# A hybrid recurrence and convolution layer on one core: where the modulation sums leave their bank, the order of the first squares, and the place of the gate sums

## The chip, the core and the metric

The kernel runs on one core of a Trainium2 chip. The core has a matrix engine (PE; PEld is its loading of weights), a vector engine (DVE), a scalar engine (ACT), a general engine (POOL) and a sequencer that issues most transfers (SP). The metric is the device time of one execution in microseconds. Three runs of the kernel before took 2156.95 to 2159.48 us, median 2158.66.

## What is computed

One layer over 2048 latent tokens `x` of width 1024, with 256 context tokens `ctx` in front (in short form):

```python
shift, scale, gate = split(silu(c) @ w_ada + b_ada, 3)          # and the same from c_ctx
h  = rmsnorm(x, norm_w) * (1 + scale) + shift                   # hc from ctx likewise
p  = h @ w_in                                                   # 1024 -> 9216 columns
pc = hc @ w_in[:, :5120]
# 8 heads of 128: q, v, forward and backward forget gates, output gate;
# a gated linear recurrence in both directions, which starts from the context's final states
y_hg = rms(o) * onorm_w * silu(p_gate)
# 1024 channels: u = cg * h_, a convolution over 3 neighbours in rows of 64
y_cv = bg * conv3(u) * silu(p_cgate)
y = concat(y_hg, y_cv) @ w_out
out = rmsnorm(x + gate * y, final_norm_w)
```

`shift` and `scale` are needed before anything else can be multiplied with `w_in`; `gate` is needed only at the very end, in the residual addition.

## The kernel before

**Tiling.** The tokens stand in four groups of 512 (`NG = 4`), the model width in eight blocks of 128 partitions (`KT = 8`, `HK = 4`). Large products are made of float16 pairs (a high and a low part), three matmuls for each product, and by a scheme of seven block products in place of eight (`seven`). The operands of a group for that scheme are the seven "hop" tiles B11, T1, T2, B21, T3, B22, T4. They are built once, stored to device memory (`Hd0` to `Hd3`), and loaded again (`hop_tile`) for each stretch of work that uses that group. Groups 0 and 1 are first used in a plain form (`plain`), and their T products are built later, by the eight "late turns" (`late_turn`), which read the saved rows `Xd` back.

**Stages.** The opening computes the sums for `shift` and `scale` (`modulate`, bank `pada`, 128x512), copies them out and transposes them (`modulate_end`), adds the bias (`ada`), and makes from them the columns `ab` with which every transposed row of the tokens is scaled and shifted (`affine`, `rows`). For group 0 the raw transposed rows already stand in SBUF (`raw`); so `rows` only scales them in place, on DVE for the first four blocks and on ACT for the last four. Then `turn` makes the high and low parts.

After that runs a list of windows (`stretch`): head 0 by its four token groups (windows 0 to 3), head 1 by its four groups in reverse order (windows 4 to 7), and so on, then the convolution and the output. Window 0 also multiplies the context. Each window has its products on PE (`units`), a chain of steps for the scan of the segment before (`scan_steps`, `context_steps`), and extra steps.

**What sets the order.** Each step has a weight (`PACE`, `paced`). The two lists of a window are merged by the share of their weight done (`merge_steps`), and `run` issues a step when the products have come that far. Instructions are written down in this order with a priority, and a scheduler then fixes each engine's queue before the run; it may draw an instruction forward when its inputs and its buffer are free. So an engine's queue is fixed and runs in order, but not always in the order of the list. `follow` pins some instructions behind a given one on their engine.

**The extra steps of windows 0 to 2.** For each following group there are five lists from `norm_group`: loads, squares and `norm` (the sum of squares by ACT, then a reciprocal root by small DVE steps, then the scaling, split between DVE and ACT), turns, late turns, and rows made ahead. In window 0 the order is: the context's squares and norm (`ctx_norm[1]`), its turns, the loads of group 2, the squares and norm of group 1 (`n1[1]`), its turns. In window 2, group 3 is turned, each turn with the next turn's rows ahead. Windows 3 to 6 make two late turns each.

**Gate sums.** `gate_sums` loads the third 1024 columns of `w_ada` in eight tiles of 512 KB (`wg`, in tiles of the pool that holds the Q tiles, six slots), multiplies each with the conditioning columns `sc32` into one bank, copies the bank out and stores it (`Gr`) for the end. Before, it is an extra list of window 3: two loads, then by turns one `part` and one load.

**Pools.** Three banks of PSUM serve transposes and the scan's level products (`pa_t`), two serve values, keys, states and scales (`px_t`), three the large products (`bank`).

**Loads of hop tiles.** `prefetch` keeps a queue of the hop tiles that windows will need, in order, nine slots in all. It issues a load when a slot is free and the group's operands are ready (`ready`, `late_done`). Windows 3 and 4 share group 3; window 5 loads group 2 again.

Of the kernel before, what the change touches and what calls it, by code (L numbers as in the profile page):

```python
# [14 lines left out]
AF = mybir.ActivationFunctionType  # L15
ALU = mybir.AluOpType
# [5 lines left out]
KT = D // P  # L22
# [4 lines left out]
NG = SEQ // GW  # L27
NCH = GW // P
HK = KT // 2
HW = GW // 2  # L30
# [20 lines left out]
def paced(weight, fn):  # L51

    return PACE.get(weight, weight), fn


def sub(t, off, dims):
    return bass.AP(t.tensor, t.offset + off, [list(t.ap[0])] + [list(d) for d in dims])
# [3 lines left out]
def hybrid_layer(ctx: ExitStack, tc, x, cx, w_ada, b_ada, w_in, w_out, fnorm_w, small_d, masks, ident_d, sel_d, out):  # L61
    nc = tc.nc
    V, S, G, PE, SY = nc.vector, nc.scalar, nc.gpsimd, nc.tensor, nc.sync
# [30 lines left out]
    def pa_t(nm):  # L94
        return pa.tile([P, 512], F32, tag="pa", name=nm)

    def px_t(nm):
        return px.tile([P, 512], F32, tag="px", name=nm)

    def ring(nm):  # L100
        return rp.tile([P, GW], F32, tag="ring", name=nm)
# [61 lines left out]
    par, at = {}, 0  # L163
# [8 lines left out]
    ab = cp.tile([P, 2, 2, KT], F32, name="ab")  # L172
# [39 lines left out]

    def modulate_end(pada):
        ada_r = ring("ada_r")
        V.tensor_copy(ada_r[:, :HW], pada[:, :HW])
        S.activation(ada_r[:, HW:], pada[:, HW:], AF.Copy)
        ptr = pa_t("ada_t")
        turned = [PE.transpose(ptr[:, q * P:(q + 1) * P], ada_r[:, q * P:(q + 1) * P], ident) for q in range(4)]
        V.tensor_tensor(ada, ptr.rearrange("p (q j m) -> p j q m", q=4, j=4)[:, :, :, 0:2],
                        sub(bada, 0, [[4, 4], [1, 4], [0, 2]]), ALU.add)  # L220
        return turned
# [20 lines left out]
    def norm_group(ntile, src, row0, m, nm, first_ops=None, space=q_tile):  # L242
# [29 lines left out]
        def transposed(k, space=pa_t):  # L272
            pt = space(f"xT_{nm}{k}")
            for i in range(ntile):
                PE.transpose(pt[:, i * P:(i + 1) * P], xs[i][:, k * P:(k + 1) * P], ident)
            return pt
# [9 lines left out]
        def rows(k):  # L286
            if k in raws:
                h32 = raws[k]
                if k < HK:
                    V.tensor_scalar(h32, h32, ab[:, m, 0, k:k + 1], ab[:, m, 1, k:k + 1], ALU.mult, ALU.add)  # L290
                else:
                    S.activation(h32, h32, AF.Identity, bias=ab[:, m, 1, k:k + 1], scale=ab[:, m, 0, k:k + 1])
                return h32
            pt = transposed(k)
            h32 = ring(f"h32_{nm}{k}")
            S.activation(h32[:, :n], pt[:, :n], AF.Identity, bias=ab[:, m, 1, k:k + 1], scale=ab[:, m, 0, k:k + 1])
            return h32
# [776 lines left out]
    def gate_sums():  # L1074

        pg, wa = [], {}

        def load(k):
            wa[k] = flat(q_tile(f"wg{k}"))
            SY.dma_start(wa[k], w_ada[0, k * P:(k + 1) * P, 2 * D:])  # L1080

        def part(k):
            if k == 0:
                pg.append(pa_t("gate_r"))
            for j in range(2):
                r = 64 * (k % 2) + 32 * j
                PE.matmul(pg[0][r:r + 32, :], sc32[:, k, :], wa[k][:, j * 512:(j + 1) * 512],
                          start=k < 2, stop=k >= KT - 2)

        def rows():  # L1090
            r = ring("gate_rows")
            S.activation(r, pg[0], AF.Copy)
            SY.dma_start(Gr, r)

        steps_ = [lambda: load(0), lambda: load(1)]
        for k in range(KT):
            steps_.append(lambda k=k: part(k))
            if k + 2 < KT:
                steps_.append(lambda k=k: load(k + 2))
        return [paced(1.0, f_) for f_ in steps_ + [rows]]  # L1100

    def gate_steps():
        t = {}
# [123 lines left out]
    for wi, (kind, a, i) in enumerate(stretch):  # L1227
        units, chain, extra = [], [], []
# [147 lines left out]
    queue = []  # L1376
    freed = [0]
    taken = [0]
    ready = [0]
# [3 lines left out]

    def prefetch():
        while (queue and taken[0] < freed[0] + HOPS and queue[0][1] <= ready[0]
               and late_done.get(queue[0][1], HK) == HK):
            wi_, g_, o = queue.pop(0)
            t = hop_tile(f"hop{wi_}{o}")
            SY.dma_start(t, Hd[g_][o])
            hop.setdefault(wi_, {})[o] = t  # L1390
            taken[0] += 1

    late_done = {0: 0, 1: 0}
    plain = [[hp.tile([P, 2, 2, GW], F16, tag="hop", name=f"hop{g}_{i}") for i in range(KT // 2)] for g in range(2)]
    x1_norm = norm_group(NCH, x, GW, 0, "x1", plain[1], stage_tile)
# [5 lines left out]
    first = norm_group(NCH, x, 0, 0, "x0", plain[0])  # L1401
# [9 lines left out]
    pada = modulate(lambda k: first[4][k]() if k < KT - 2 else None, lambda: next_w(0))  # L1411
    ctx_norm = norm_group(2, cx, 0, 1, "c")
# [11 lines left out]
    def store_plain(g):  # L1424
        for o in ("B11", "B21", "B22"):
            r, half = int(o[1]) - 1, int(o[2]) - 1
            for i in range(HK // 2):
                SY.dma_start(Hd[g][o][:, 2 * i:2 * i + 2],
                             plain[g][r * HK // 2 + i][:, :, :, half * HW:(half + 1) * HW])
# [107 lines left out]
    for wi, (units, chain, extra) in enumerate(windows):  # L1537
        if wi < NG - 1:
            n1 = x_norm[wi + 1]
            n2 = x_norm[wi + 2] if wi + 2 < NG else None  # L1540
            ready_ = [paced(0.0, lambda g=wi + 1: set_ready(g))]
            if wi == 0:
                more_params()
                early = ([paced(0.1, lambda: store_plain(0))] + ctx_norm[1] + ctx_norm[2] + n2[0] + n1[1] + n1[2]
                         + [paced(0.1, lambda: next_w(1, 6))] + n2[1] + ready_)
            elif wi == 1:
                x3 = [st for _, st in n2[0]]
                early = ([paced(0.1, lambda: store_plain(1))] + n1[2][:2] + [paced(0.0, x3[0]), paced(0.0, x3[1])]
                         + n1[2][2:3] + [paced(0.0, x3[2]), paced(0.0, x3[3])] + n2[1][:2] + n1[2][3:] + ready_
                         + n2[1][2:] + n2[5][:1])  # L1550
            else:
                early = [st for k in range(HK) for st in n1[2][k:k + 1] + n1[5][k + 1:k + 2]] + ready_
            extra = early + extra
        elif wi < NG + 3:
            n_ = (wi - NG + 1) * 2
            extra = (x1_norm[3] + first[3])[n_:n_ + 2] + extra
        if wi == NG - 1:
            extra = extra + gate_sums()
        if wi >= NG:
            ready[0] = NG  # L1560
        run(wi, units, merge_steps(chain, extra))
        if stretch[wi] == ("conv", 0, 1):
            close_scan()
        elif stretch[wi] == ("conv", 0, 3):
            afterwards.append(close_heads)
        elif stretch[wi] == ("pair", 7, 0):
            load_wo(0, 6)
            afterwards.append(lambda: load_wo(6, 7))
        elif stretch[wi] == ("pair", 7, 1):
            afterwards.append(lambda: load_wo(13, 14))  # L1570
# [113 lines left out]
```

## Time and profile before

| | us |
|---|---|
| median of three runs | 2158.66 |
| profiled execution | 2153.81 |
| its span | 2152.0 |
| PE busy | 2076.1 (96% of the span) |
| DVE busy | 1645.7 (76%) |
| ACT busy | 1192.0 (55%) |
| POOL busy | 184.7 (9%) |
| mean granted clock of PE | 0.994 |

The profiled execution is a single one; its own time is its span and 1.81 us around it. In the rows of the views, a time in square brackets is the idle time of the engine just before the instruction, with what ended it. "x4" means four instructions in a row merged into one line. In a row by tile, three numbers with slashes are the shortest, the median and the longest duration in ns. The granted clock is a share of PE's full speed. An instruction on PE, DVE or ACT starts a little before the end of the one ahead, so durations in a row add up to slightly more than the time they take.

### The profile page before, as it was taken

What the parts mean: (1) busy time and instruction counts of PE and PEld (TensorE: products, weight loads), DVE (VectorE), ACT (ScalarE), POOL (GpSimd) and SP (SyncE); (2) the same over time, 40 slices, a digit from 0 to 9 for tenths busy, and PEclk for the clock granted to TensorE, in tenths of its full rate; (3) what the DMA queues carried; (4) which work ended last, traced back from release to release, by engine and by line L of the source; (5) the groups of instructions that cost most, each with busy time, mean ns of one, the idle gap of its engine ahead of it and who ended that gap; (6) DMA issues with size and microseconds to landing.
All of it is one profiled execution on the core that took longest, in us unless ns stands there. A gap on an engine that the chain in (4) does not pass through costs nothing.

```text
span 2152.0 us, 53038 instructions
## 1 busy us (share of the span) xinstructions
PE 2076.1 (96%) x22111; PEld 1466.1 (68%) x22111; DVE 1645.7 (76%) x3415; ACT 1192.0 (55%) x2406; POOL 184.7 (9%) x271
## 2 busy tenths in 40 slices
PE   5988999999999999999999999999999999999998
PEld 2777778888888888888888887444444444444443
DVE  7787888878778787788787887678778656687775
ACT  6965666766567666667676654354445423333332
POOL 0121111011111110111110100000000000000000
PEclk8999999999999999999999999999999999999999
DMA  9557544442243333423633457933442105642421
GB/s 359 181 174 259 181 153 147 138 139 90 97 147 131 112 114 109 136 98 129 207 130 125 132 164 258 288 108 109 136 147 94 55 22 196 206 144 90 137 79 59
DMA packets 185797, 311.01 MB, mean 145 GB/s; under 512 B 13010, under 2 KB 114770, under 8 KB 183764
## 3 DMA queue, kind: packets, MB, share of 16 engines
q1 hardware_dynamic: 183396, 303.68, 42.6%
q8 instruction: 173, 2.83, 0.5%
q10 hardware_dynamic: 2160, 3.93, 0.5%
q14 instruction: 68, 0.56, 0.1%
HBM read 240.19 MB, written 67.37 MB: 143 GB/s over the span
## 4 chain that ended last, share of the span: by engine, by line
PE 64%; DVE 18%; ACT 8%; DMA 4%; issue 3%; POOL 1%; SPq 0%; POOLq 0%; ACTq 0%; DVEq 0%
PE sa L930 8%; PE sa L932 8%; PE sa L931 8%; PE sb L930 4%; PE sb L931 4%; PE sb L932 4%; PE sa_o L930 2%; PE sa_o L931 2%; PE sa_o L932 2%; DVE Q L492 2%; PE sc L930 2%; PE sc L931 2%; PE sc L932 2%; PE T L681 2%; DVE K L485 2%
## 5 line engine op out<-in xcount | busy, mean ns | idle before, releaser
L931 PEld LDWEIGHTS <-e_p 128*128 128x128 f16 x1332 | 130.3, 98 | 57.3 <-issue 8.1
L930 PEld LDWEIGHTS <-e_p 128*128 128x128 f16 x1332 | 130.3, 98 | 56.2 <-issue 3.6
L485 DVE TENSOR_TENSOR K<-K,tot 128x512 f32<-128x512 f32 x192 | 133.0, 693 | 45.7 <-ACT km L601 28.2
L932 PEld LDWEIGHTS <-e_p 128*128 128x128 f16 x1332 | 130.3, 98 | 51.0
L601 ACT ACTIVATE km<-K 128x512 f32<-128x512 f32 x192 | 129.6, 676 | 62.0 <-DVE K L485 58.2
L492 DVE TENSOR_TENSOR Q<-Q,tot 128x512 f32<-128x512 f32 x192 | 132.9, 692 | 35.5 <-POOL qm L608 19.4
L608 POOL COPY qm<-Q 128x512 f32<-128x512 f32 x96 | 79.1, 824 | 796.4 <-DVE Q L492 796.4
L931 PEld LDWEIGHTS <-whib_p 128*128 128x128 f16 x888 | 87.2, 98 | 39.7 <-issue 6.2
L930 PEld LDWEIGHTS <-whib_p 128*128 128x128 f16 x888 | 87.1, 98 | 37.9 <-issue 1.7
L931 PEld LDWEIGHTS <-whia_p 128*128 128x128 f16 x888 | 86.9, 98 | 36.7 <-issue 4.6
L932 PEld LDWEIGHTS <-wlob_p 128*128 128x128 f16 x888 | 87.1, 98 | 34.1
L930 PEld LDWEIGHTS <-whia_p 128*128 128x128 f16 x888 | 86.9, 98 | 34.1 <-issue 0.8
L932 PEld LDWEIGHTS <-wloa_p 128*128 128x128 f16 x888 | 86.9, 98 | 34.0
L157 ACT ACTIVATE e_p<-ws_p,sc_p 128x512 f16<-128x512 f32 x108 | 77.5, 719 | 53.8 <-DVE ws_p L444 39.2
L665 POOL COPY A<-Ac 32x128 f32<-32x128 f32 x128 | 75.8, 593 | 128.9 <-ACT A L661 119.4
L937 ACT ACTIVATE u<-sa,sx_w 128x256 f32<-128x256 f32 (+1 forms) x111 | 58.1, 524 | 47.2 <-PE sa L932 38.2
L853 ACT ACTIVATE cv<-c,small 128x512 f32<-128x512 f32 (+1 forms) x36 | 24.2, 673 | 106.0 <-DVE c L871 60.8
L937 ACT ACTIVATE p<-sa,sx_w 128x256 f32<-128x256 f32 (+1 forms) x111 | 57.5, 518 | 42.2 <-PE sa L932 42.2
L409 ACT ACTIVATE junk<-ws_p 128x1024 f16<-128x1024 f32 x72 | 75.7, 1052 | 5.7 <-DMA ws_p<-in_w_in 5.5
L158 DVE SCALAR_TENSOR_TENSOR e_p<-ws_p,sc_p,e_p 128x512 f16<-128x512 f32 x108 | 78.7, 743 | 0.0
L1595 POOL TENSOR_TENSOR x_o<-x_o,fw 128x512 f32<-128x512 f32 x1 | 1.3, 1262 | 868.4 <-ACT junk L1586 868.4
L937 ACT ACTIVATE p<-sb,sx_w 128x256 f32<-128x256 f32 (+1 forms) x111 | 57.9, 521 | 31.1 <-PE sb L932 28.5
(858 smaller groups left out, 7029.7 us busy)
## 6 DMA issues: line engine op xcount, KB each, us to landing
ws_p<-in_w_in SPq DMA_DIRECT2D x72, 512.0 KB, 4.3
y_o<-yT SPq DMA_DIRECT2D x32, 512.0 KB, 4.3
xt_x<-in_x SPq DMA_DIRECT2D x16, 512.0 KB, 5.9
wa<-in_w_ada SPq DMA_DIRECT2D x16, 512.0 KB, 10.2
Gd<-zs SPq DMA_DIRECT2D x32, 256.0 KB, 2.8
sg<-Gd SPq DMA_DIRECT2D x32, 256.0 KB, 3.9
wos<-in_w_out SPq DMA_DIRECT2D x32, 256.0 KB, 4.8
yT<-y SPq DMA_DIRECT2D x32, 256.0 KB, 2.7
```

Of the source, the lines that this page charges most:

```text
L157: S.activation(hi, src, AF.Copy, scale=st[:, 0:1])
L158: V.scalar_tensor_tensor(lo, src, st[:, 0:1], hi, ALU.mult, ALU.subtract)
L409: S.activation(junk.rearrange("p (k n) -> p k n", k=KT), stage[i], AF.Abs, accum_out=r)
L485: V.tensor_tensor(m, m, sub(cur, nb + 1, [[2, np_], [-(nb + 1), 2], [0, B]]), ALU.mult)
L492: V.tensor_tensor(m, m, sub(cur, 1, [[2, np_], [nb - 1, 2], [0, B]]), ALU.mult)
L601: S.activation(sub(s.km, 0, [[2 * B, n // (2 * B)], [B, 2], [1, B]]), mix(s.K, n, B, n // (2 * B)), AF.Copy)
L608: G.tensor_copy(sub(qm, 0, [[2 * B, n // (2 * B)], [B, 2], [1, B]]), mix(s.qf, n, B, n // (2 * B)))
L665: G.tensor_copy(A3[js, :, js], s.Ac[js])
L930: PE.matmul(ps, hi[:, k], rh, start=start and k == 0, stop=False, skip_group_check=not start)
L931: PE.matmul(ps, hi[:, k], right(name, 1, k), start=False, stop=False, skip_group_check=not start)
L932: PE.matmul(ps, lo[:, k], rh, start=False, stop=k == nk - 1, skip_group_check=not start)
L937: last_keep.append(S.activation(r, ps, AF.Copy, scale=sx))
```

## The change

Four edits, all within the first seven windows:

1. `modulate_end` copies the whole bank of modulation sums with one ACT copy instead of a DVE half and an ACT half.
2. In `rows`, the raw row `k == HK - 2` (that is k = 2, group 0 alone) is scaled by POOL instead of DVE.
3. In window 0 the four squares of group 1 stand right behind the context's squares, ahead of the context's norm, and group 1's norm stands behind the context's first turn instead of behind all four.
4. The gate sums become three steps of window 2: four loads; four parts and the next four loads; four parts and the copy out with its store. Their bank comes from the two-bank pool. The late turns are shared out as 3, 2, 1, 2 over windows 3 to 6, and hop tiles for windows from the fifth on are not loaded before `ready` has reached four, which is set at the start of window 4.

```diff
     def modulate_end(pada):
         ada_r = ring("ada_r")
-        V.tensor_copy(ada_r[:, :HW], pada[:, :HW])
-        S.activation(ada_r[:, HW:], pada[:, HW:], AF.Copy)
+        S.activation(ada_r, pada, AF.Copy)
...
                 if k < HK:
-                    V.tensor_scalar(h32, h32, ab[:, m, 0, k:k + 1], ab[:, m, 1, k:k + 1], ALU.mult, ALU.add)
+                    eng = G if k == HK - 2 else V
+                    eng.tensor_scalar(h32, h32, ab[:, m, 0, k:k + 1], ab[:, m, 1, k:k + 1], ALU.mult, ALU.add)
...
             if k == 0:
-                pg.append(pa_t("gate_r"))
+                pg.append(px_t("gate_r"))
...
-        steps_ = [lambda: load(0), lambda: load(1)]
-        for k in range(KT):
-            steps_.append(lambda k=k: part(k))
-            if k + 2 < KT:
-                steps_.append(lambda k=k: load(k + 2))
-        return [paced(1.0, f_) for f_ in steps_ + [rows]]
+        def some(fn, k0):
+            for k in range(k0, k0 + HK):
+                fn(k)
+
+        return [paced(0.1, lambda: some(load, 0)),
+                paced(1.0, lambda: (some(part, 0), some(load, HK))), paced(1.0, lambda: (some(part, HK), rows()))]
...
         while (queue and taken[0] < freed[0] + HOPS and queue[0][1] <= ready[0]
-               and late_done.get(queue[0][1], HK) == HK):
+               and late_done.get(queue[0][1], HK) == HK and (queue[0][0] < NG or ready[0] == NG)):
...
-                early = ([paced(0.1, lambda: store_plain(0))] + ctx_norm[1] + ctx_norm[2] + n2[0] + n1[1] + n1[2]
+                early = ([paced(0.1, lambda: store_plain(0))] + ctx_norm[1][:-1] + n1[1][:-1] + ctx_norm[1][-1:]
+                         + ctx_norm[2][:1] + n1[1][-1:] + ctx_norm[2][1:] + n2[0] + n1[2]
                          + [paced(0.1, lambda: next_w(1, 6))] + n2[1] + ready_)
...
-                early = [st for k in range(HK) for st in n1[2][k:k + 1] + n1[5][k + 1:k + 2]] + ready_
+                sums = gate_sums()
+                early = (sums[:1] + [st for k in range(HK) for st in n1[2][k:k + 1] + n1[5][k + 1:k + 2] + sums[k:k + 1] * (k > 0)]
+                         + ready_)
             extra = early + extra
         elif wi < NG + 3:
-            n_ = (wi - NG + 1) * 2
-            extra = (x1_norm[3] + first[3])[n_:n_ + 2] + extra
-        if wi == NG - 1:
-            extra = extra + gate_sums()
+            at = (0, 3, 5, 6, 8)[wi - NG + 1:]
+            extra = (x1_norm[3] + first[3])[at[0]:at[1]] + extra
```

## The prediction

> **What bounds the kernel now.** I read the page first, then busy time by stretch, then the matrix engine's waits in the early stretches, then the rows of each engine around the lines that the change touches. "Window" below is one entry of the kernel's list of stretches (one head by one token group). Their borders are read from the PE rows: window 0 from 42.4, window 1 from 83.7, window 2 from 138.6, window 3 from 182.4 to 235.
>
> ```profile
> span 2152.0 us, 53038 instructions
> PE 2076.1 (96%) x22111; PEld 1466.1 (68%) x22111; DVE 1645.7 (76%) x3415; ACT 1192.0 (55%) x2406; POOL 184.7 (9%) x271
> ```
>
> PE is busy 96% of the span, so only its 76 us of idle time and the matmuls at a low clock can be won, unless matmuls are removed. The change removes none. Busy time by stretch (bounds, length, then PE, PE loads, DVE, ACT, POOL, granted clock, DMA share, GB/s):
>
> ```profile
> 0.00:42.40 42.40, 22.09 (x103) 7.94 (x104) 27.33 (x71) 28.31 (x47) 0.65 (x5) 0.92 0.92 356
> 42.40:83.70 41.30, 37.38 (x313) 31.73 (x313) 30.52 (x83) 35.44 (x62) 8.62 (x16) 0.92 0.71 243
> 83.70:138.60 54.90, 47.73 (x637) 40.30 (x634) 49.84 (x127) 41.96 (x75) 12.61 (x15) 1.00 0.49 150
> 138.60:182.40 43.80, 39.79 (x575) 35.03 (x576) 36.59 (x76) 27.56 (x50) 8.46 (x15) 1.00 0.61 207
> 182.40:235.00 52.60, 48.29 (x600) 34.82 (x599) 36.57 (x81) 30.24 (x57) 6.58 (x9) 0.97 0.69 245
> ```
>
> PE idles 20.3 us before window 0, then 3.9, 7.2, 4.0 and 4.3 us in windows 0 to 3. Window 1 is DVE's (91% busy), windows 2 and 3 are PE's, with DVE at 84% and 70%. Everything the change edits lies here.
>
> **Part by part. Modulation sums (A).** Before, the left half leaves by DVE, the right by ACT.
>
> ```profile
> 33.53 2.83 PE L206 MATMUL pada<-wa,sc 128*32 128x512 f32 x14
> ...
> 38.10 0.91 PE L218 MATMUL ada_t<-ident,ada_r 128*128 128x128 f32 x4 [1.16 <-DVE ada_r L215]
> ```
>
> ```profile
> 36.43 1.28 DVE L282 COPY h_x<-xT_x 128x512 f32<-128x512 f32 x2
> 37.63 0.41 DVE L215 COPY ada_r<-pada 128x256 f32<-128x256 f32 x1
> 39.05 0.19 DVE L219 TENSOR_TENSOR ada<-ada_t,small 128x32 f32<-128x32 f32 x1 [1.01 <-PE ada_t L218]
> ```
>
> ```profile
> 35.19 0.58 ACT L284 ACTIVATE h_x<-xT_x 128x512 f32<-128x512 f32 x1
> 38.14 0.38 ACT L216 ACTIVATE ada_r<-pada 128x256 f32<-128x256 f32 x1 [2.37 <-DVE ada_r L215]
> ```
>
> The sums end at 36.36. DVE reaches its half only at 37.63, behind two copies, and ACT, idle since 35.77, waits for it. One ACT copy of 128x512 costs 0.58 (the L284 row), so 36.36 to 36.98; four transposes 0.91; DVE's addition can start at 37.93, after its copies end at 37.71. That is 1.1 us before 39.05, and affine, the rows and the first matmul follow in a chain. No cover is used up: ACT's next work waited for these transposes anyway. **A = -1.1.**
>
> **One affine row on POOL (B).** One instruction only: the row k=2 of group 0.
>
> ```profile
> L290 DVE TENSOR_SCALAR h_x<-h_x,ab x4: 540/726/935, 41.0 to 44.4; 128x512 f32<-128x512 f32 x4
> ...
> L301 POOL TENSOR_SCALAR hop<-h_x x4: 618/682/752, 42.0 to 45.6; 128x512 f16<-128x512 f32 x4
> ...
> L312 DVE TENSOR_TENSOR hop<-h_x,hop x8: 672/678/1093, 42.8 to 48.6; 128x512 f16<-128x512 f32 x8
> ```
>
> DVE sheds 0.54 (the undisturbed L290). POOL's form with two column operands has no row; nearest is its cast, 0.62 to 0.75, and POOL is free until 41.95. But DVE rows stretch by 0.40 (L290, 935 against 540) and 0.42 (L312, 1093 against 678) when a POOL cast runs beside them. Bounds: -0.5 (nothing blocked) to +0.6 (a second DVE row blocked as well, and POOL's own cast 0.7 later with DVE waiting for it). I take the nearest rows, 0.54 less 0.4: **B = -0.1.** The Trainium skill, page "SBUF — State Buffer", section "Who interferes with whom", speaks against this edit: GpSimd and a DVE instruction with two SBUF inputs share a port pair that is locked for a whole instruction; by it B would be 0.54 less 0.68, thus +0.1.
>
> **Squares of group 1 ahead (C).** Nothing is added; two of four squares move ahead of the context's scaling, and group 1's rsqrt ahead of three context turns.
>
> ```profile
> 52.65 1.15 ACT L266 ACTIVATE xt_c<-xt_c,rsy_c 128x1024 f32<-128x1024 f32 x1 [2.01 <-DVE rsy_c L137]
> 53.70 1.04 ACT L257 ACTIVATE junk<-xt_x 128x1024 f16<-128x1024 f32 x1
> ...
> 59.84 1.08 ACT L257 ACTIVATE junk<-xt_x 128x1024 f16<-128x1024 f32 x1
> ```
>
> ```profile
> 61.04 0.17 DVE L131 TENSOR_SCALAR rsv_x<-ssq_x 128x4 f32<-128x4 f32 x1 [0.52 <-ACT junk L257]
> ```
>
> ```profile
> 67.26 0.44 PE L275 MATMUL xT_x<-ident,xt_x 128*128 128x128 f32 x2 [1.54 <-DVE xt_x L268]
> ```
>
> ```profile
> 74.10 0.27 PE L1491 MATMUL u<-hc,whia_p 128*128 128x256 f16 x1
> ...
> 88.25 0.44 PE L555 MATMUL vt_c<-ident,vT_c 128*128 128x128 f32 x2 [1.49 <-ACT vT_c L550]
> ```
>
> ACT stands idle 2.01 us before the context's scaling. The two squares (1.04 to 1.08 and a read of 0.2 each, 2.4 us together) fit there but for 0.4, by which ACT's half of the context's scaling is later. In return the last square ends near 53 instead of 60.9, and group 1's rsqrt starts about 7 us earlier, long before PE wants its transposes. So the wait of 1.54 goes, and ACT has 2.4 us less to do up to 88, where PE waited 1.49 for it. Behind the squares on ACT stand the context's rows; the context's units start only at 74. Bounds: +0.4 (only the delay counts) to -3.0 (both waits go). I take the first wait whole and a third of the second, since window 1 belongs to DVE: **C = -2.0.**
>
> **Gate sums (D).** Eight loads of 512 KB and eight pairs of matmuls move from window 3 to window 2, loads in fours; the bank comes from the two-bank pool; loads of hop tiles for windows past the fourth wait until window 4; window 3 takes three late turns instead of two, window 5 one.
>
> ```profile
> 226.51 1.05 PE L1087 MATMUL gate_r<-wg,sc 128*32 128x512 f32 x4
> ...
> 227.50 0.28 PE L930 MATMUL sc<-hop3B,whia_p 128*128 128x256 f16 x1
> ```
>
> ```profile
> 178.56 0.33 SPq L326 DMA_DIRECT2D Hd3T<-hpT_x  x1
> 178.94 0.42 SPq L1080 DMA_DIRECT2D wg<-in_w_ada  x1
> 179.46 0.40 SPq L1389 DMA_DIRECT2D hop3B<-Hd3B  x1
> ```
>
> ```profile
> 185.19 0.27 PE L930 MATMUL sa<-hop3B,whia_p 128*128 128x256 f16 x1 [2.49 <-DMA hop3B<-Hd3B]
> ```
>
> ```profile
> 185.20:189.20 4.00, 4.00 (x23) 2.99 (x23) 0.00 (x0) 0.72 (x2) 0.00 (x0) 0.59 0.91 312
> ```
>
> The matmuls cost 0.98 a pair (226.51 to 227.50), 7.9 us in all, wherever they stand: zero in the sum. What counts is the waits. At the border to window 3 PE waits 2.49 us for the first hop tile, whose load stands behind a gate load on SP. Then it runs four microseconds at a mean clock of 0.59, which is 0.41 x 4.0 = 1.6 us more. Without the gate load ahead, the hop load is issued 0.5 earlier and has 512 KB less before it (1.5 us at the 356 GB/s of the first stretch): 2.0 of 2.49. Besides, the second block of gate matmuls (3.9 us) now stands between group 3's last transposes and the window's end, while DVE builds the operands that are to be stored; so the rest goes too, and with it the low clock: -4.1. The Trainium skill, "TensorE: Matmul & The Clock Gate", section "What's actually happening", lets the clock drop only after an idle window of about 3.4 us; by that D would lose 1.6 of its gain, but here a gap of 2.49 was followed by the low clock.
>
> ```profile
> PE gate_r L1087 <- DMA wg<-in_w_ada: 0.8, 1, 0.8
> ```
>
> ```profile
> L321 DVE TENSOR_TENSOR hpT_x<-ht_x,hpT_x 128x512 f16<-128x512 f32 x2 | 1.4, 692 | 0.6 <-ACT hpT_x L303 0.5
> L321 DVE TENSOR_TENSOR hpT_x<-hb_x,hpT_x 128x256 f16<-128x256 f32 x2 | 0.8, 422 | 0.7 <-POOL hpT_x L301 0.7
> ```
>
> The 0.8 that PE waited for a gate load in window 3 falls away. Against it: a third late turn puts on DVE one row of 0.69 and six of 0.42, 3.2 us, while window 3 shrinks to 52.6 - 7.9 - 4.1 - 0.8 = 39.8 us. DVE then has 36.6 + 3.2 = 39.8: the window is as much DVE's as PE's. Window 2, with PE at 47.7 and DVE at 36.6, gains slack instead. From the windows shown, PE idles 4.0 where DVE has 84%; at 100% it could be 7. I charge 2.0 (bounds 0 to 4.5). The two-bank pool is held only between the blocks, 48% to 74% of window 2 by the step weights, while the key turn that needs it comes at 78%; if the copy out slipped, that turn would wait up to 3.9. The held-back loads cost nothing: window 5 starts at 276.
>
> ```profile
> 121.25 0.76 PE L275 MATMUL xT_x<-ident,xt_x 128*128 128x128 f32 x5
> ```
>
> ```profile
> 119.39 0.33 SPq L253 DMA_DIRECT2D xt_x<-in_x  x1
> 128.79 0.52 SPq L324 DMA_DIRECT2D Hd2T<-hpT_x  x1
> ```
>
> The first four loads (2 MB, 6 us) need the Q slots of group 2, free after its last transposes at 121.25 to 122.0, and SP has nothing until 128.79, so I cost them at nothing. **D = -4.1 - 0.8 + 2.0 = -2.9.**
>
> **Sum:** -1.1 - 0.1 - 2.0 - 2.9 = -6.1 us on the profiled execution's 2153.81 (span 2152.0 and 1.81 around it), so 2147.7. The median of the runs shown, 2158.66, lies 4.85 above that execution; the forecast for the median is 2158.66 - 6.1 = **2152.6 us**.
>
> **Rivals.** *R1, window 3 turns to DVE:* three late turns and two weight splits in a window of 39.8 us leave 4.5 us idle, and D is -0.4. For it: 39.8 against 39.8; against: at that window's start DVE stood idle 5.88 us in one piece, because the low clock held PE up.
>
> ```profile
> 190.12 0.69 DVE L794 TENSOR_TENSOR zs<-z,zs 128x512 f32<-128x512 f32 x1 [5.88 <-ACT zs L793]
> ```
>
> Time 2158.66 - 3.6 = 2155.1. *R2, the start is absorbed:* window 1 is 91% DVE, and moving its inputs does not shorten its work; A to C give 0.5 instead of 3.2. Against: DVE idles 10.8 us in window 0, waiting for exactly these inputs. Time 2155.3. *R3, slower:* the second four loads come too late for the second block. Each is issued when a matmul pair of the first block frees its slot, with 26% of window 2 (11.4 us) until the block.
>
> ```profile
> DMA to landing us min/median/max: 3.5/4.4/5.4
> ```
>
> Four loads need 4.4 and three times 1.5, 8.9 us; if the stores of group 3 and the weight loads take 2.5 us of the queue, or PE's order puts the block earlier, PE waits. Price: 4.4 for the first, 0.5 for each further (1.5 less 0.98), 5.9; the low clock after it 1.6; and the loads lie before group 3's stores, so the 4.1 at window 3 isn't won; 2.0 for DVE stays. D = +5.9 + 1.6 - 0.8 + 2.0 = +8.7, with A to C +5.5: 2164.2. Decided where the loads start less than 8.9 us ahead. *R4, nothing moves:* the new list order leaves each engine's order as it was, because instructions already run ahead of the list (of group 1's four squares only two stand behind the context's scaling). Only A and B act: 2157.5.
>
> **How the numbers follow.** Forecast 0.58, with its own range 2147 to 2154.3; R1 0.15, R2 0.08, R3 0.12, R4 0.07. About 0.2%, 4.3 us, is what a measurement of this kernel tells from no change; faster therefore means under 2154.3. The forecast's case gives faster 0.56 and R1 and R2, which lie close to the border, 0.05 between them: 0.61. Slower is R3 and a little of R4: 0.13. The rest, 0.26, is no change. The range 2145 to 2160 leaves out R3 and the best end, where both of C's waits and all of D's go and DVE costs nothing.
>
> **What would show it.** Right: the addition after the sums at about 38; no wait for group 1's scaled tiles near 66; no wait for a hop tile at the border of window 3, and no clock below 1 there; gate matmuls in two blocks of four pairs. Wrong: a PE wait for a gate load in window 2 (R3), a window 3 longer than 43 us with PE waiting for DVE (R1), or window 1 longer by what the start gained (R2).

## The result, and the profile after

The changed kernel took **2147.51 us** (median of four runs, 2146.27 to 2151.83), the kernel before on the same chip 2159.07: a ratio of 0.995 with a 95% interval of 0.9935 to 0.9966, about 11.6 us faster. Measured again beside the last experiments (five runs) it took 2150.38, ratio 0.9961 (0.9948 to 0.9973). Over all nine runs the median is 2148.7, 10.0 us under the 2158.66 from which the forecast started. The forecast was 2152.6, so the direction was right and the gain was some 4 us larger than its sum. The profiled execution is the slowest of the first four: 2151.83.

The page of the kernel after, its span and its engines:

```profile
span 2150.1 us, 53050 instructions
PE 2073.2 (96%) x22111; PEld 1466.0 (68%) x22111; DVE 1645.8 (77%) x3413; ACT 1192.2 (55%) x2406; POOL 191.8 (9%) x272
```

PE executes as many instructions as before and is busy 2.9 us less; the prediction had left cheaper matmuls out ("The change removes none"). Busy time by stretch of the kernel after, with the same columns as before:

```profile
0.00:41.20 41.20, 21.34 (x103) 7.50 (x104) 26.97 (x70) 28.50 (x47) 1.39 (x5) 0.96 0.92 353
41.20:81.70 40.50, 37.67 (x311) 31.89 (x311) 31.67 (x82) 35.52 (x63) 10.34 (x17) 0.92 0.76 261
81.70:136.60 54.90, 47.86 (x640) 40.53 (x637) 49.46 (x126) 41.62 (x75) 12.35 (x15) 1.00 0.59 188
136.60:184.40 47.80, 44.58 (x599) 36.03 (x600) 36.98 (x75) 28.01 (x50) 9.26 (x15) 0.96 0.68 242
184.40:230.00 45.60, 38.57 (x559) 32.53 (x558) 35.02 (x76) 29.00 (x55) 9.03 (x10) 1.00 0.62 207
```

The start is 1.2 us shorter, window 0 0.8, window 1 unchanged, window 2 longer by 4.0 and window 3 shorter by 7.0. The last border is not the same in both: the first large product of window 4 begins at 233.4 in the kernel before and at 230.2 in the kernel after, so 235.0 was 1.6 late, and up to these rows window 3 is 5.2 shorter. The gate matmuls have left window 3 and stand in window 2, but the 7.9 us that they took in window 3 have not become 7.9 in window 2. The rows of PE of the kernel after, in order of time, say why:

```profile
136.96 2.12 PE L274 MATMUL xT_x<-ident,xt_x 128*128 128x128 f32 x8 [1.55 <-DVE xt_x L267]
...
160.18 1.92 PE L1087 MATMUL gate_r<-wg,sc 128*32 128x512 f32 x16
...
171.22 1.92 PE L1087 MATMUL gate_r<-wg,sc 128*32 128x512 f32 x16
...
187.22 0.28 PE L930 MATMUL sa<-hop3B,whia_p 128*128 128x256 f16 x1 [2.06 <-DMA hop3B<-Hd3B]
```

Four pairs in a block take 1.92 us, 0.48 a pair; before, each pair stood alone and took 0.98 to 1.05. All eight take 3.84 us instead of 7.9. The last row shows what did not happen: PE still waits 2.06 us for the first hop tile of window 3. SP's issues of the kernel after, in order:

```profile
161.28 1.77 SPq L1080 DMA_DIRECT2D wg<-in_w_ada  x4
...
178.07 0.53 SPq L324 DMA_DIRECT2D Hd3T<-hpT_x  x1
178.69 1.25 SPq L324 DMA_DIRECT2D Hd3B<-hpB_x  x2
181.23 0.33 SPq L326 DMA_DIRECT2D Hd3T<-hpT_x  x1
182.88 0.33 SPq L1389 DMA_DIRECT2D hop3B<-Hd3B  x1
```

No gate load stands at the border any more, but group 3's last stores are issued 2.5 us later than before (178.07 against 175.55), and the hop load 3.4 later (182.88 against 179.46).

### The profile page after: what moved, and what is told of

Same layout as the page of the kernel before. It is cut to its first block, busy times and chain, and to the rows that moved or that the text cites. A ratio compares the mean times of both kernels' runs of the same rounds, so it can differ in the third digit from the quotient of the medians.

```text
span 2150.1 us, 53050 instructions
## 1 busy us (share of the span) xinstructions
PE 2073.2 (96%) x22111; PEld 1466.0 (68%) x22111; DVE 1645.8 (77%) x3413; ACT 1192.2 (55%) x2406; POOL 191.8 (9%) x272
## 4 chain that ended last, share of the span: by engine, by line
PE 65%; DVE 18%; ACT 7%; DMA 4%; issue 3%; POOL 1%; SPq 0%; POOLq 0%; ACTq 0%; DVEq 0%
PE sa L930 8%; PE sa L932 8%; PE sa L931 8%; PE sb L930 4%; PE sb L932 4%; PE sb L931 4%; PE sa_o L930 2%; PE sa_o L931 2%; PE sa_o L932 2%; DVE Q L492 2%; PE sc L930 2%; PE sc L931 2%; PE sc L932 2%; DVE K L485 2%; PE T L681 2%
## 5 line engine op out<-in xcount | busy, mean ns | idle before, releaser
L157 ACT ACTIVATE e_p<-ws_p,sc_p 128x512 f16<-128x512 f32 x108 | 77.5, 718 | 54.9 <-DVE ws_p L444 42.0
```

What stands on the lines that cost most here:

```text
L157: S.activation(hi, src, AF.Copy, scale=st[:, 0:1])
```

## The experiments

Each ran with five rounds beside the kernel before on the same chip; all ratios are to that kernel, whose median was 2158.64, 2159.81 and 2159.65 us in the three sets.

**Both halves of the bank in turn.** The question was whether neighbouring pairs run side by side because they write different quarters (32 rows each) of the bank.

```diff
-                r = 64 * (k % 2) + 32 * j
+                r = 64 * (k // HK) + 32 * j
...
-                          start=k < 2, stop=k >= KT - 2)
+                          start=k % HK == 0, stop=k % HK == HK - 1)
```

> The kernel after, but all four pairs of a gate block write the same two quarters of the bank (the first block rows 0 to 63, the second rows 64 to 127), so that neighbouring pairs can't run side by side in different column quarters of the array. Quarters theory: sixteen gate records take 3.9 us instead of 1.92 in each block, PE's busy time rises by about 3.9 us, and the kernel is 3 to 4 us slower than the kernel after. Place theory (the gain comes from where loads and matmuls stand): the blocks and the time stay as in the kernel after, within 1 us.

2151.42 us, ratio 0.997 (0.9958 to 0.9981). The gate rows of PE in this version:

```profile
158.13 3.63 PE L1087 MATMUL gate_r<-wg,sc 128*32 128x512 f32 x16
...
170.68 3.63 PE L1087 MATMUL gate_r<-wg,sc 128*32 128x512 f32 x16
```

Same place, same loads, same number of instructions; only the rows of the bank that neighbours write differ, and a block takes 3.63 instead of 1.92. The halving is shown in the rows: 3.4 us for both blocks. In the time this version lies 3.9 us above the first median of the changed kernel and 2.7 above that of its nine runs, but its interval overlaps both of the changed kernel, so the time alone does not settle it.

**Blocks, but in window 3.** The new loads, blocks and bank in the kernel before, with the list left in window 3.

```diff
-                pg.append(pa_t("gate_r"))
+                pg.append(px_t("gate_r"))
...
-        return [paced(1.0, f_) for f_ in steps_ + [rows]]
...
+        return [paced(0.1, lambda: some(load, 0)),
+                paced(1.0, lambda: (some(part, 0), some(load, HK))), paced(1.0, lambda: (some(part, HK), rows()))]
```

> The kernel before with the gate sums as three steps (four loads; four parts and four loads; four parts and the copy out) from the two-bank pool, but still in window 3. Quarters theory: PE's gate time falls from 7.9 to 3.9 us and the kernel is 3 to 4 us faster than before, unless the four loads push the hop tiles of group 3 back. Place theory: no gain, and a longer wait for the first hop tile of window 3 (four gate loads ahead of it instead of one, 2.5 us growing to 5 or more), so 0 to 5 us slower than before.

2161.47 us, ratio 1.0014 (1.0006 to 1.0023): slower. Its PE rows:

```profile
187.38 0.37 PE L930 MATMUL sa<-hop3B,whia_p 128*128 128x256 f16 x1 [3.25 <-DMA hop3B<-Hd3B]
...
223.77 1.05 PE L1087 MATMUL gate_r<-wg,sc 128*32 128x512 f32 x4
225.62 1.05 PE L1087 MATMUL gate_r<-wg,sc 128*32 128x512 f32 x4
```

Written as a block, the pairs were drawn apart by the scheduler, each took 1.05 as before, and the wait at the border grew from 2.49 to 3.25. So the place decides whether the block comes about: in window 2 the blocks stayed whole. No gate load stands ahead of the hop load in this version (SP issues it at 180.82, behind a store at 179.89), and still the wait is longer than before.

**Part D alone, and parts A to C alone.** The kernel before with the gate part of the diff only (first diff, its core), and with the opening's edits only (second).

```diff
...
+                sums = gate_sums()
+                early = (sums[:1] + [st for k in range(HK) for st in n1[2][k:k + 1] + n1[5][k + 1:k + 2] + sums[k:k + 1] * (k > 0)]
...
```

```diff
+        S.activation(ada_r, pada, AF.Copy)
...
+                    eng = G if k == HK - 2 else V
...
+                early = ([paced(0.1, lambda: store_plain(0))] + ctx_norm[1][:-1] + n1[1][:-1] + ctx_norm[1][-1:]
...
```

> The kernel before with edit D alone (gate sums in window 2, two-bank pool, late turns 3, 2, 1, 2, hop loads held back). As predicted: 2.9 us faster than before. Quarters theory: about 4 us faster, all of it in PE's gate time. If D is the larger part of what was measured (11.6 us between the medians), 7 us or more.

> The kernel before with edits A, B and C and without D. As predicted: 3.2 us faster than before. By the trace of the kernel after, whose window 1 begins 2.0 us earlier: 2 us faster. If the start is absorbed by window 1: 0 to 0.5 us.

D alone: 2150.54 us, ratio 0.9968 (0.9955 to 0.998), that is 6.9 us by the ratio (4.3 to 9.7) and 8.1 between the medians. A to C alone: 2155.45, ratio 0.9985 (0.9977 to 0.9994), 3.2 us (1.3 to 5.0). The two ratios take 0.47% off, the whole change 0.39 to 0.5%: the parts add up within their intervals, and the surplus over the forecast lies in D.

**Without the squares ahead.** The changed kernel with window 0's old order.

```diff
-                early = ([paced(0.1, lambda: store_plain(0))] + ctx_norm[1][:-1] + n1[1][:-1] + ctx_norm[1][-1:]
-                         + ctx_norm[2][:1] + n1[1][-1:] + ctx_norm[2][1:] + n2[0] + n1[2]
+                early = ([paced(0.1, lambda: store_plain(0))] + ctx_norm[1] + ctx_norm[2] + n2[0] + n1[1] + n1[2]
```

> The changed kernel with the order of window 0's extra steps as it was before (squares of group 1 behind the context's norm). Theory, the prediction's term C: +2.0 us against the changed kernel, 2149.5, with the last square of group 1 back at about 58 and the wait of 1.5 for group 1's scaled tiles back on PE. Rival: in the trace of the changed kernel the scheduler left two squares behind the context's scaling as before (54.88 for the last), so the order gave little of its own: window 1 begins only 0.84 earlier relative to window 0's first matmul. By that +0.3 to +0.8 us, 2147.8 to 2148.3.

2152.58 us, ratio 0.9968 (0.9956 to 0.9981). ACT's rows of the changed kernel in order of time:

```profile
52.33 1.15 ACT L265 ACTIVATE xt_c<-xt_c,rsy_c 128x1024 f32<-128x1024 f32 x1 [2.84 <-DVE rsy_c L137]
53.39 1.04 ACT L256 ACTIVATE junk<-xt_x 128x1024 f16<-128x1024 f32 x1
...
54.88 1.04 ACT L256 ACTIVATE junk<-xt_x 128x1024 f16<-128x1024 f32 x1
```

The last of these rows, of ACT, in the version without the new order:

```profile
62.20 1.09 ACT L256 ACTIVATE junk<-xt_x 128x1024 f16<-128x1024 f32 x1
```

and the wait of PE in it:

```profile
68.32 0.44 PE L274 MATMUL xT_x<-ident,xt_x 128*128 128x128 f32 x2 [2.01 <-DVE xt_x L267]
```

The last square falls from 54.88 to 62.20 and the wait for group 1's tiles is back, at 2.01. Window 1 begins at 85.01 instead of 81.98, 3.0 us later in the two profiles. But behind that wait this version has a low clock, which the changed kernel does not have there (1.00 over the same stretch):

```profile
66.00:73.00 7.00, 4.99 (x30) 4.00 (x28) 2.77 (x11) 4.23 (x6) 0.52 (x1) 0.76 0.06 22
```

0.24 of 7.0 us is 1.7 us; without it some 1.3 is left, between the theory's 2.0 and the rival's 0.3 to 0.8. In the time the intervals of this version and of the changed kernel's second measurement overlap. The rival's observation holds too: even in the changed kernel both squares stand behind the context's scaling, and ACT's idle time ahead of it grew from 2.01 to 2.84. What the new list order did was to keep the last square from sliding behind the context's rows.

**The POOL row back on DVE.**

```diff
-                    eng = G if k == HK - 2 else V
-                    eng.tensor_scalar(h32, h32, ab[:, m, 0, k:k + 1], ab[:, m, 1, k:k + 1], ALU.mult, ALU.add)
+                    V.tensor_scalar(h32, h32, ab[:, m, 0, k:k + 1], ab[:, m, 1, k:k + 1], ALU.mult, ALU.add)
```

> The changed kernel with the raw row k=2 of group 0 back on DVE. Theory, the prediction's term B: +0.1 us, not to be told from nothing. Rival: the rows of DVE beside POOL are stretched (four rows of L312 in 4.13 us in the changed kernel, where a row undisturbed takes 0.68), so the row on POOL costs: then -0.3 to -0.6 us at the end of DVE's rows, with less than 3.6 us for those four rows.

2149.49 us, ratio 0.9956 (0.9942 to 0.9969), not to be told from the changed kernel. DVE's rows in the changed kernel:

```profile
41.53 4.13 DVE L312 TENSOR_TENSOR hop<-h_x,hop 128x512 f16<-128x512 f32 x4
...
46.93 1.28 DVE L312 TENSOR_TENSOR hop<-h_x,hop 128x512 f16<-128x512 f32 x2
```

and DVE's rows in this version:

```profile
43.23 0.91 DVE L289 TENSOR_SCALAR h_x<-h_x,ab 128x512 f32<-128x512 f32 x1
44.06 4.10 DVE L311 TENSOR_TENSOR hop<-h_x,hop 128x512 f16<-128x512 f32 x6
```

With the row on POOL four subtractions take 4.13, 1.03 each; without it six take 4.10. Both sets end at the same time (46.93 + 1.28 = 48.21; 44.06 + 4.10 = 48.16). The row that DVE sheds is lost again in stretched rows: in these rows B is nothing.

**No hold on the hop tiles (first diff), and two late turns in each window (second).**

```diff
-               and late_done.get(queue[0][1], HK) == HK and (queue[0][0] < NG or ready[0] == NG)):
+               and late_done.get(queue[0][1], HK) == HK):
```

```diff
-            at = (0, 3, 5, 6, 8)[wi - NG + 1:]
+            at = (0, 2, 4, 6, 8)[wi - NG + 1:]
```

> The changed kernel without the condition that holds hop tiles of windows from the fifth on back until window 4. Theory (the prediction costed the hold at nothing): 0 +- 1 us, 2147.5. Rival: the loads of window 4's and 5's tiles are issued in window 3 ahead of loads that window 3 needs, and take the transfer engines at its start: the wait for the first hop tile at window 3 (2.06 us) grows by 1 to 3 us and may be followed by a low clock, 2149 to 2152.

> The changed kernel with two late turns in each of windows 3 to 6, as before, in place of 3, 2, 1, 2. Theory, the prediction's charge of +2.0 for DVE in window 3: -2.0 us, 2145.5, and the PE waits for DVE and ACT rows in window 3 (1.15, 1.25, 0.57) go. Rival: window 3 isn't bound by DVE; the waits stay and the third turn of window 3 only shifts work: 0 us, or up to +2 where window 5 then waits for a late turn.

No hold: 2153.09 us, ratio 0.9974 (0.9962 to 0.9986). Two late turns: 2152.36, ratio 0.9969 (0.9958 to 0.9981). Both intervals overlap that of the changed kernel's second measurement, so neither difference (2.8 and 1.7 us by the ratios) is established. The theory of the second, a gain of 2.0 by taking a late turn out of window 3, is refuted as far as this can show; PE's waits in its window 3 remain:

```profile
202.79 0.27 PE L930 MATMUL sb<-hop3T,whib_p 128*128 128x256 f16 x1 [1.30 <-DVE f L941]
210.13 0.27 PE L930 MATMUL sa<-hop3T,e_p 128*128 128x256 f16 x1 [1.52 <-ACT u L937]
213.94 0.65 PE L657 MATMUL A<-Q,K 128*32 128x64 f32 x32 [1.80 <-DVE Q L492]
```

They are waits for steps of the scan and of the products' ends, 4.6 us with two late turns as with three (4.7). The version shows one thing more: window 5, from its first hop tile to that of window 6, takes 34.3 us with two late turns and 32.2 with one (34.4 in the kernel before), and window 6 31.4 instead of 32.1. Without the hold the wait at the border was 2.61 instead of 2.06, with no low clock behind it.

**The changed kernel again, and its second block moved to the border.** Its control on one more chip, and two orders: the second block behind group 3's last turn (first diff), and besides the first block behind group 3's last transposes and the second at the window's end (second diff).

```diff
-                early = (sums[:1] + [st for k in range(HK) for st in n1[2][k:k + 1] + n1[5][k + 1:k + 2] + sums[k:k + 1] * (k > 0)]
-                         + ready_)
+                early = (sums[:1] + [st for k in range(HK) for st in n1[2][k:k + 1] + n1[5][k + 1:k + 2]
+                                     + sums[1:2] * (k == 1) + sums[2:] * (k == 3)] + ready_)
```

```diff
+                early = (sums[:1] + [st for k in range(HK) for st in n1[2][k:k + 1] + n1[5][k + 1:k + 2]
+                                     + sums[1:2] * (k == 2)] + ready_ + sums[2:])
```

> The changed kernel itself, on the chip of the runs beside it, so that what single parts are worth can be read without a change of chip. If its four runs so far were typical: 2147 to 2149 us, ratio 0.994 to 0.996, 2 to 5 us below the versions that lack one part. If they were lucky: ratio 0.996 to 0.997, no more than 2 us below the versions that lack the hold of hop tiles or the uneven late turns.

> The changed kernel with the second block of gate matmuls not right behind group 3's last transposes but at the end of window 2, where PE waits 2.06 us for the first hop tile of window 3. Theory (the store of group 3's last operands and the load behind it set that wait, and any matmul that is ready can fill it): the block of 1.92 us goes into the wait, the last transposes and the stores stay where they are or come earlier, the wait falls to under 0.6 us, and the time by 1.5 to 2 us against the changed kernel. Rival: the copy out of the bank and the states behind it move into the border too, or the bank that is held longer keeps the states waiting: no gain, and a wait for the two-bank pool near 80 to 95% of window 2.

> As the run before, and the first block too stands behind group 3's last transposes. Theory: transposes and stores of group 3 come 1.9 us earlier, but the second four gate loads (2 MB, 6 us at the transfer rate of the opening) are now issued at 172 instead of 161, among and ahead of group 3's stores and window 3's loads. So the wait at the border is for a gate load or a hop tile, 2 to 6 us, and the time 1 to 5 us above the run before. Rival: the transfer engines have room (0.6 of their time used here), the loads are hidden, and it is the fastest of all, another 0.5 to 1 us below the run before.

The changed kernel again: 2150.38 us, ratio 0.9961 (0.9948 to 0.9973), between the two cases of its expectation; the first four runs were on the quick side. Second block at the border: 2149.6, ratio 0.9958 (0.9946 to 0.9971). Both late: 2148.68, ratio 0.9953 (0.994 to 0.9965). Neither is told apart from the changed kernel. PE's rows of the version with the second block at the border:

```profile
180.84 1.04 PE L1087 MATMUL gate_r<-wg,sc 128*32 128x512 f32 x2
...
183.80 1.92 PE L1087 MATMUL gate_r<-wg,sc 128*32 128x512 f32 x14
...
185.99 0.27 PE L930 MATMUL sa<-hop3B,whia_p 128*128 128x256 f16 x1
```

and a DVE row of it:

```profile
184.88 1.22 DVE L567 TENSOR_TENSOR Q<-q,f 128x1024 f32<-128x1024 f32 x1 [5.01 <-PE gate_r L1087]
```

As the theory had it, no wait for a hop tile is left. But two things changed at once. The block stands at the border, and group 3's last stores are issued 3.3 us earlier than in the changed kernel, with the first block where it was:

```profile
174.73 0.52 SPq L324 DMA_DIRECT2D Hd3T<-hpT_x  x1
```

DVE's step for Q, which stands ahead of group 3's last turn in the changed kernel (172.38), is out of its way here: the gate tiles hold Q slots longer, and it waits 5.01 us until the block frees one. The scheduler also drew one matmul of the block ahead (x2 at 180.84), which takes 1.04 us alone. Window 3 begins only 1.2 us earlier than in the changed kernel (185.99 against 187.22), and the time does not show more than 0.8 us.

With both blocks late the wait at the border was 0.30 us: the second four loads, issued at 170.29, arrived in time. The theory, which had them in the way, was wrong; the rival (room on the transfer engines) was right. Here the hop load is issued at 181.66, 1.2 us earlier than in the changed kernel, and the second block, at 185.25 for 1.92 us, stands where PE had waited.

**Two pairs at a time in the old place.** The kernel before, with loads and parts issued two by two.

```diff
-        for k in range(KT):
-            steps_.append(lambda k=k: part(k))
-            if k + 2 < KT:
-                steps_.append(lambda k=k: load(k + 2))
+        for k in range(0, KT, 2):
+            if k + 2 < KT:
+                steps_.append(lambda k=k: (load(k + 2), load(k + 3)))
+            steps_.append(lambda k=k: (part(k), part(k + 1)))
```

> The kernel before, with its gate matmuls issued and loaded two pairs at a time in their old place in window 3. Where two pairs stand next to each other on PE they write all four quarters of the bank. Theory (neighbours on different quarters run side by side): two such pairs take 0.96 instead of 1.96 us; the scheduler keeps two of the four couples together, so -2.0 us against the kernel before, 2156.7. Rival (a pair costs 0.98 wherever it stands, as the prediction had it): 0, and loads that come two at a time cost up to +1.

2158.24 us, ratio 0.9997 (0.9988 to 1.0006): no change. Its PE rows:

```profile
209.86 1.04 PE L1087 MATMUL gate_r<-wg,sc 128*32 128x512 f32 x8
211.92 1.05 PE L1087 MATMUL gate_r<-wg,sc 128*32 128x512 f32 x4
...
228.15 1.05 PE L1087 MATMUL gate_r<-wg,sc 128*32 128x512 f32 x4 [1.38 <-DMA wg<-in_w_ada]
```

Two pairs side by side take 1.04 us, one pair alone 1.05: half of the bank's quarters idle in the lone pair. Two of the four couples stayed together, 2.0 us of PE. The time hardly shows it: here PE waits 1.38 instead of 0.82 for a gate load, 2.91 instead of 2.49 at the border, and 1.92 instead of 0.99 for other engines in window 3.

## Why the prediction was right or wrong

**A (-1.1): right, in size and mechanism.** ACT's row of the kernel after:

```profile
36.35 0.60 ACT L215 ACTIVATE ada_r<-pada 128x512 f32<-128x512 f32 x1 [0.60 <-PE pada L206]
```

and DVE's:

```profile
37.90 0.19 DVE L218 TENSOR_TENSOR ada<-ada_t,small 128x32 f32<-128x32 f32 x1 [0.21 <-PE ada_t L217]
```

The addition starts at 37.90 (forecast 37.93) instead of 39.05, and the first matmul of window 0 is 1.15 earlier.

**B (-0.1): right.** It is 0.0. The Trainium skill, "SBUF — State Buffer", section "Who interferes with whom", says that a DVE instruction with two SBUF inputs contends with a GpSimd instruction that reads SBUF; the rows agree (1.03 a subtraction while POOL is at work, 0.64 in the pair behind it).

**C (-2.0): one wait right, the way not, the size open.** The wait of 1.54 for group 1's tiles is gone. Window 1 begins at 81.98 instead of 83.98; 1.15 of these 2.00 us are A's, so in these rows adding C won 0.85. Undoing it cost 3.0, of which 1.7 is a low clock. And the two squares did not go into ACT's idle 2.01 ahead of the context's scaling, and the wait of 1.49 for the context's values, of which a third was counted, stayed at 1.47. R4's observation, that the scheduler and not the list sets ACT's order, was half right. A to C together measured 3.2 (1.3 to 5.0), as summed; R2 falls, since window 1 kept its 54.9 us and began 2.0 earlier.

**D (-2.9): one term was set at zero and is 4 us.** The step "The matmuls cost 0.98 a pair ... wherever they stand: zero in the sum" failed. The cost of a pair depends on its neighbour: back to back, four neighbouring pairs write all four quarters of the bank and run side by side. A row of the kernel before had it in plain sight, the modulation sums of the opening, which are the same shape in the same four quarters:

```profile
19.64 2.41 PE L206 MATMUL pada<-wa,sc 128*32 128x512 f32 x16
22.28 1.05 PE L206 MATMUL pada<-wa,sc 128*32 128x512 f32 x4 [0.23 <-DMA wa<-in_w_ada]
```

Sixteen in 2.41, four in 1.05: 0.60 a pair in company, 1.05 alone; in the blocks it became 0.48. The version that changes nothing but the quarters (3.63 a block instead of 1.92) shows this cause in the rows. The Trainium skill, "TensorE: Matmul & The Clock Gate", section "Part 3: Packing small matmuls — row/col tiling", has the rule: matmuls that use fewer than 128 columns of the array and stand at different tile positions run concurrently. The blocks agree: 0.91 a pair on two quarters, 0.48 on four.

*The border to window 3 (-4.1): wrong, -0.4.* The wait fell from 2.49 to 2.06 only. The step that failed is "the second block ... now stands between group 3's last transposes and the window's end ... so the rest goes too". The block was issued right behind those transposes (171.22), nothing of it lay near the border, and the last stores came 2.5 us later, behind the first block and a low clock at the window's start. With the second block at the border the wait went, but the stores came earlier there too, so what the block did alone is not told apart. The other step, that the gate load ahead of the hop load makes 2.0 of the 2.49, failed as well: none stands there in the changed kernel, and none in the version with the blocks in window 3, where the wait is 3.25.

*The low clock (1.6 of the 4.1).* It is gone at this border, although a wait of 2.06 is there. It came instead behind a wait of 1.55 at 136.96 (1.26 in the second profile of the changed kernel). Stretches of the changed kernel around both, with columns as before:

```profile
136.00:143.00 7.00, 5.86 (x33) 4.55 (x34) 3.38 (x7) 5.65 (x8) 0.62 (x1) 0.76 1.00 392
185.00:192.00 7.00, 4.94 (x45) 4.16 (x43) 1.87 (x3) 3.03 (x7) 0.00 (x0) 1.00 0.96 315
```

0.24 of 7.0 us is 1.7 us: what the one border won the other lost.

*The gate load's wait (-0.8): right*, no PE row waits for a gate load, and R3 falls with it. *DVE in window 3 (+2.0): too small, and the reason wrong.* Leave out the waits at the border and for a gate load, which the sum counts elsewhere. Then PE waited once in window 3 of the kernel before:

```profile
212.78 0.65 PE L657 MATMUL A<-Q,K 128*32 128x64 f32 x32 [0.99 <-DVE Q L492]
```

In the kernel after it waits 4.7 us in all, 3.7 more, for ACT, DVE and POOL by turns. The longest of these waits:

```profile
203.12 0.27 PE L930 MATMUL sa<-hop3T,e_p 128*128 128x256 f16 x1 [1.15 <-ACT p L937]
...
204.75 0.27 PE L930 MATMUL sb<-hop3T,whib_p 128*128 128x256 f16 x1 [1.25 <-DVE f L941]
...
211.61 0.52 PE L650 MATMUL A<-qm,km 128*32 128x64 f32 x18 [1.48 <-POOL qm L608]
```

That is inside the bounds of 0 to 4.5, but the third turn does not make them: with two they are 4.6. What the record points to is a cost that the prediction left out. The lone gate pairs were ready work between these steps (at 204.59 and 209.97, among others). The waits are 0.99 us in both profiles that have them there one by one (the kernel before, and A to C alone), 1.92 with couples, and 2.7 to 4.8 in all eleven without them or with them only from 223.77 on. That the pairs filled the waits is read from this; no run tried it by itself. So about half of what the lone pairs cost PE had been hidden. R1 is half there: window 3 is longer than the 43 us named as its sign.

**The sum for the median.** Put 4.0 for the matmuls into D and leave the rest: 6.1 + 4.0 = 10.1, which is the 10.0 of the nine runs. That agreement is luck. It hides 3.7 too much at the border, 1.7 too little for the waits in window 3, and windows 5 and 6, which the prediction did not count and which are 1.6 shorter together.

The rows can be added up by the lead of the changed profile. It is 2.0 us at the first matmul of window 1 (A to C), 4.3 at the first hop tile of window 5 (268.4 against 272.7) and 5.9 at that of window 7 (332.7 against 338.6). D's 2.3 up to window 5 are 4.1 for the matmuls, 0.8 for the gate load, 0.4 at the border and 1.1 for a shorter wait in window 2 (0.65 instead of 1.78), less 3.7 for the waits in window 3 and some 0.4 elsewhere. So in the rows the whole change is worth 5.9, close to the forecast's 6.1, by errors that cancel. The 4 us from there to the 10.0 of the medians are not placed: the one profile of the kernel before ran 4.85 us under its median, and where its slower executions lose their time is not recorded.

**The profiled executions.** Up to 627 us the changed profile leads by 5.9; at its end only by 2.0. Most of the loss, 3.6, is in one place, near 1035 us, far from every edit. PE's wait there in the kernel before:

```profile
1041.65 0.46 PE L631 MATMUL A<-qm,km 128*32 128x32 f32 x32 [1.34 <-POOL qm L608]
```

and in the kernel after:

```profile
1039.02 0.46 PE L631 MATMUL A<-qm,km 128*32 128x32 f32 x32 [2.66 <-POOL qm L608]
```

The stretch around it by engine, in the kernel before:

```profile
1030.00:1046.00 16.00, 14.39 (x250) 12.55 (x251) 9.29 (x21) 14.85 (x44) 1.72 (x2) 1.00 0.89 304
```

and in the kernel after:

```profile
1030.00:1046.00 16.00, 12.40 (x268) 9.83 (x266) 8.23 (x15) 11.09 (x31) 1.74 (x2) 0.89 0.63 209
```

PE's waits there are 3.6 instead of 1.6 in all, and the low clock, 0.11 of 16.0 us, makes 1.8. The wait alone does not go with the change: it is 1.34 to 2.38 us in the four profiles without D in window 2, 1.48 to 2.66 in the ten with it. The clock does: over the 16 us it is 1.00 in all four, and 0.82 to 0.89 in nine of the ten (1.00 in the version without the squares ahead). So this loss is no chance of one execution, and if these are typical the medians hold it too; how D leads to it is open. ACT waited 2.04 us for a load of the output weights just ahead of it in the changed profile and 0.22 in the one of before; that this load sets the wait is argued from the order of the rows and was not tried. The profile of before, at 2153.81 us, is under each of the other 49 runs of its kernel beside the experiments (2155.01 at the lowest). So the medians, not the two profiles, tell the gain.

## What to carry to other kernels

Before costing a move of small matmuls at zero, look for rows of the same shape in other company: what a matmul on a quarter of the array's columns costs depends on which quarter its neighbour uses. Ask also what else such lone matmuls do: where they are ready work between dependent steps, moving them lays waits bare. A block that is written as one may be drawn apart by the scheduler, so its place has to be read from the rows. Judge a change of half a per cent by medians of many runs, since the profile of one execution may lie 4.85 us from the median, as that of the kernel before did.

## What the runs showed of the hardware

Matmuls of 128x32 float32 weights by 512 columns: one pair on two quarters alone takes 1.05 us, two pairs on four quarters 1.04, four pairs 1.92, and four pairs on two quarters 3.63.

Whether a low clock follows a wait isn't set by the wait's length in this kernel: after 1.55 us at 136.96 the clock was 0.76 over 7 us, after 2.06 at 187.22 it was 1.00, and in the version with the second block at the border a wait of 1.55 at the former place left it at 1.00:

```profile
136.00:143.00 7.00, 5.27 (x43) 4.12 (x42) 4.04 (x15) 5.48 (x8) 0.62 (x1) 1.00 0.96 355
```

Nor is it a matter of one execution: at the border to window 3 a low clock followed in all four profiles without D in window 2 (waits of 2.49 to 3.25) and in none of the ten with it (none to 2.61). So the price of a low clock cannot be read from a wait's length alone. The Trainium skill, "TensorE: Matmul & The Clock Gate", section "What's actually happening", says that the activity window is free-running. The two outcomes after 1.55 us agree with that; no run here shows the window itself.
